# Gated linear scans in a decoder layer: all eight sample states of a head multiplied in one run of passes, and three blocks of values turned by 32x32 blocks and DMAs in place of TensorE transposes

## The chip, the cores and the metric

One core of one Trainium2 chip runs the whole program. The metric is the device time of one execution in microseconds (us). The kernel before takes 2281.77 us, the median of three runs (2281.49 to 2285.34). The engines are named as in the profile: PE (TensorE; PEld is its loading of weights), DVE (VectorE), ACT (ScalarE), POOL (GpSimd) and SP (SyncE, which here only issues DMAs).

## The reference

One layer with two feed-forward blocks (FFN1, FFN2) and between them a mixer of recurrent heads, for 256 prompt tokens and for 32 sample tokens (8 sequences of 4). The mixer has 4 GLA heads (keys of 128, values of 256) and 8 HGRN heads (keys of 128, values of 128). Each head is a scan with its own state S of keys by values:

```python
S_t = diag(a_t) S_{t-1} + k_t^T v_t      # a_t, k_t, q_t: 128 wide; v_t: 256 or 128 wide
o_t = q_t S_t
```

The prompt starts from a zero state. Each of the 8 sample sequences starts from a state of its own, which is an input, so a head has eight sample states. Outputs are the layer's result for both groups of tokens and the final states. The projections are `h @ w_in`, where values v are one part of the columns.

## The kernel before, in words

**Layout.** Activations lie with features on the 128 partitions and the 288 tokens (256 prompt, 32 sample) along the free axis: 16 tiles `x`, 16 tiles `y`, and for the matmuls `xh` and `xl`, the high and low part of x. Weights arrive over SP's queue in units of 512 KB (`raw`), ACT rounds each into `wh` (L96), DVE makes the rest `wl` (L97), and each product is three matmuls of 288 columns (L548, L549, L550). `Weights` keeps 3 raw units and 4 split units ahead.

**Order.** `block` (L539) computes 512 output features: for each of 16 input tiles k it issues 4 x 3 = 12 matmuls, then calls `tick(k)`. In the mixer, `tick` (L1284) carries the scans along under the projections: it takes one item from `turns`, then advances the first scan's generator one step, then runs what `later` holds. So a step of a scan stands in PE's queue between two groups of 12 matmuls. The queues of the engines are in order; a framework lays out the instructions of each engine from the program's order and sets the semaphores.

**Blocks in the mixer.** qk0, v0, qk1, v1 for the two GLA pairs of heads, then hfq0, hi0, hfq1, hi1, hfq2, hfq3 for the four HGRN pairs, then four gate blocks. v0, v1, hi0 and hi1 make the values, 512 features each, and each scan works on two heads (a = 0, 1). The six scans run under the block after the one that completes their inputs.

**Values** (`ev_v`, L882). The scans need values with tokens on the partitions. As each of a block's four feature tiles f is done, DVE multiplies its 256 prompt columns by the norm `rt` into a tile y (L887) and three copies of its 32 sample columns into `v3` (L888), and one turn is put on `turns`. A turn is three PE transposes into a PSUM tile `tp_v` (L866 twice, L867 for the three copies), an ACT copy into `Vt` (L895), an ACT copy of the sample part into `V32` (L896), and the stacked high, low and high parts `Vs` (ACT L871, DVE L873). With four blocks there are 16 turns.

**Scan** (`scan`, L910). Eight levels build the decayed scores (`Dg`, `Ds`, `X`). From the third last step on, and at each sample step, `load_state` (L929) puts one 256 KB DMA of sample states on SP's queue: 2 states for GLA, 4 for HGRN, 5 buffers in all. Then for each of the two heads:

- `out(a)` (L1158): PE multiplies values and scores into `po` for the prompt, and into `ss` for the samples (L1169 stands last of these).
- `sample(a, b0)`, four times for GLA (2 states each) and twice for HGRN (4 states each): the update `sn` from keys and values (L1191 or L1194); for each state b a product of the queries `qm` (32 columns as weights) with the state (256 or 128 columns) into `ss` on the 32 partitions of b % 4 (L1198); then DVE's new state (L1202) and its DMA out on POOL's queue (L1204).
- `final(a)`, `inter_a`, `inter_b`, `norm_a`: the prompt's final state, and the sum of the four groups of partitions of `ss`.

All operands of L866, L867, L1169, L1178 and L1198 are full 32-bit floats. One such matmul of L1169, L1178 or L1198 in the program appears as two in the trace (two passes); a transpose appears as one. So the 12 heads with 8 states each give 96 matmuls at L1198, 192 in the trace.

**32x32 turning in FFN2.** FFN2 has a second way to turn a tile, which the change brings to the mixer: DVE transposes each 32x32 block in place (`turn32`, L657; L660 and L662), and DMAs then carry the blocks to their rows (`move32`, L664), 16 for the prompt columns of four tiles, in 32 partitions x 8 runs of 32 floats each.

Of the kernel before, what the change touches and what calls it, by code (L numbers as in the profile page):

```python
# [16 lines left out]
P = 128  # L17
# [108 lines left out]
def trunk_kernel(ctx, tc, x_prompt, x_sample, state_gla, state_hgrn, norm_gains, f1_in, f1_out, f2_in, f2_out,  # L126
# [649 lines left out]
    def mixer(pn, border):  # L776
        with ExitStack() as mx:
# [84 lines left out]

            def by_token(tp, src, src3):

                for t in range(2):
                    PE.transpose(tp[:, t * P:(t + 1) * P], src[:, t * P:(t + 1) * P], ident)  # L866
                PE.transpose(tp[0:96, TP:TP + P], src3, ident)  # L867

# [6 lines left out]
            def vtiles(nm):  # L875
                vs32.append(vs32.pop(0))
                return (gp.tile([P, 2, 512], F32, name=f"V{nm}", tag="V"), vs32[-1],
                        gp.tile([96, 512], F32R, name=f"Vs{nm}", tag="Vs"))

            turns = []  # L880

            def ev_v(Vt, V32, Vs, y0=8):  # L882
                def ev(f, ps):

                    vt = y[y0 + f]
                    v3 = tmp.tile([P, 3, TS], F32, name="v3", tag="v3", bufs=4)
                    V.tensor_tensor(vt[:, 0:TP], ps[:, 0:TP], rt[:, 0:TP], op=ALU.mult)  # L887
                    V.tensor_tensor(v3, ps[:, TP:T].unsqueeze(1).broadcast_to([P, 3, TS]),  # L888
                                    rt[:, TP:T].unsqueeze(1).broadcast_to([P, 3, TS]), op=ALU.mult)

                    def turn():
                        tp = auxtile("tp_v")
                        by_token(tp, vt, v3.rearrange("p n t -> p (n t)"))
                        c = slice(f * P, (f + 1) * P)
                        S.activation(Vt[:, 0:2, c], tp[:, 0:TP].rearrange("p (t c) -> p t c", c=P), AF.Copy)  # L895
                        S.activation(V32[0:TS, c], tp[0:TS, TP:TP + P], AF.Copy)  # L896
                        stack(Vs[:, c], tp, TS)

                    turns.append(turn)
                return ev  # L900
# [9 lines left out]
            def scan(d, Vt, V32, Vs, gla, ytile0, s0, sp_out, ss_out):  # L910
# [18 lines left out]
                def load_state():  # L929
                    if loads:  # L930
                        a, b0 = loads.pop(0)
                        t = sp[0].tile([P, nb, dv], F32, name="s0", tag="s0", bufs=5)
                        with tc.issue_after(W.last[W.loaded - 3]):
                            nc.sync.dma_start(t, s0[b0:b0 + nb, a].rearrange("b p v -> p b v"))
                        states[a, b0] = t
# [156 lines left out]
                for step in range(LEVELS + 1):  # L1092
# [32 lines left out]
                    if step == 3:  # L1125
                        for a in range(2):
# [31 lines left out]
                def out(a):  # L1158
                    vc = Vt[:, :, a * dv:(a + 1) * dv]

                    po, ss = auxtile("o"), auxtile("os")
                    for j in range(nv):
                        vj = vc[:, :, j * P:(j + 1) * P]
                        c0, c1, c2 = j * TP, j * TP + P, (j + 1) * TP
                        PE.matmul(po[:, c0:c1], vj[:, 0, :], Dg[:, 0, a, :], start=j == 0, stop=True, skip_group_check=True)
                        PE.matmul(po[:, c1:c2], vj[:, 0, :], X[:, a, :], start=False, stop=False, skip_group_check=True)
                        PE.matmul(po[:, c1:c2], vj[:, 1, :], Dg[:, 1, a, :], start=False, stop=True, skip_group_check=True)
                        c0 = TP + j * TS
                        PE.matmul(ss[:, c0:c0 + TS], V32[:, a * dv + j * P:a * dv + (j + 1) * P], Ds[:, a, :],  # L1169
                                  start=j == 0, stop=False, skip_group_check=True)  # L1170
                    pos[a] = po, ss

                def final(a):

                    kd, vc = kds[a][0], Vt[:, :, a * dv:(a + 1) * dv]
                    ps = auxtile("st")
                    for t in range(2):
                        PE.matmul(ps[:, 0:dv], kd[:, t, :], vc[:, t, :], start=t == 0, stop=t == 1)  # L1178
                    st = tmp.tile([P, dv], F32, name="st", tag="st", bufs=1)
                    S.activation(st, ps[:, 0:dv], AF.Copy)  # L1180
                    G.dma_start(sp_out[a], st)

                def sample(a, b0):
# [9 lines left out]
                    else:  # L1193
                        PE.matmul(ps, ks, bd.rearrange("p b c -> p (b c)"), start=True, stop=True)  # L1194
                    for i in range(nb):
                        b = b0 + i
                        r = slice(b % 4 * TS, (b % 4 + 1) * TS)
                        PE.matmul(pos[a][1][r, 0:dv], qm[a][:, b * TS:(b + 1) * TS], s[:, i, :],  # L1198
                                  start=False, stop=b >= NB - 4, skip_group_check=True)
                    for i in range(nb):  # L1200
# [163 lines left out]
            for g in range(2):  # L1364
                d = group_tiles(f"g{g}")
                block(f"qk{g}", KT, xrhs, ev_gla(d, g == 0), tick=tick if g else pn.tick0, most=99 if g else 1,
                      fill=None if g else border.fill)
                if g == 0:
                    scan_pool()
                if g == 0:  # L1370
                    vt = vtiles("g0")
                    block("v0", KT, xrhs, ev_v(*vt), 
                          tick=lambda k: (pn.tick1(k), split_lr() if k == 8 else a_lr() if k == 13 else None))
                    lower_bounds()
                    gla_decay(d, g)
                else:
                    gla_decay(d, g)
                    vt = vtiles("g1")
                    block("v1", KT, xrhs, ev_v(*vt), tick=tick)
                gens.append((g, scan(d, *vt, True, 4 * g, state_gla[0][:, 2 * g:2 * g + 2],  # L1380
                                     sgp[0, 0, 2 * g:2 * g + 2], sgs[0][:, 2 * g:2 * g + 2]), True))
            ds, vts = {}, {}
            for kind, g in HORDER:
                if kind == "hi":
                    written(g)
                    vts[g] = vtiles(f"h{g}")
                    block(f"hi{g}", KT, xrhs, ev_v(*vts[g], 8 + 4 * g), tick=tick)
                else:
# [3 lines left out]
                for j in list(ds):  # L1392
                    if j // 2 in vts:
                        c = slice((j % 2) * 256, (j % 2 + 1) * 256)
                        vt, v32, vs = vts[j // 2]
                        gens.append((2 + j, scan(ds.pop(j), vt[:, :, c], v32[:, c], vs[:, c], False, 8 + 2 * j,
                                                 state_hgrn[0][:, 2 * j:2 * j + 2], shp[0, 0, 2 * j:2 * j + 2],
# [113 lines left out]
```

## Time and profile before

The profiled execution took 2281.72 us. Its span, from the first to the last instruction, is 2279.5 us.

| what | before |
|---|---|
| median of three runs | 2281.77 us |
| profiled execution, span | 2281.72 us, 2279.5 us |
| granted TensorE clock | 0.998 |
| DVE busy | 1397.6 us (61%) |
| ACT busy | 1015.4 us (45%) |
| POOL busy | 134.6 us (6%) |
| DMA mean | 168 GB/s |

The mixer takes roughly 900 to 1300 us of the span. A row of a group reads: line, engine, operation, output<-inputs, shapes, count, then busy us, mean ns of one, and idle time before. A row of the timeline reads: start in us, length in us, engine, line, operation and count; matmuls overlap, so what one costs is read from the distance between starts, and the length is modelled.

### The profile page before, as it was taken

To read this page: it belongs to the slowest core of one execution; us is meant where nothing else is said; L and a number is where in the kernel's file an instruction comes from. 1 tells how busy PE (TensorE), PEld (TensorE's weight loads), DVE (VectorE), ACT (ScalarE), POOL (GpSimd) and SP (SyncE) were. 2 spreads that over 40 slices of the span, in tenths; PEclk is the share of its full clock that TensorE was granted. 3 is DMA by queue.
4 is the path that set the end of the run, shared out by engine and by line. 5 is a ranking of instruction groups with operands and counts; after the bars stand their busy time and mean duration, and the time that the engine had idled before them with its cause. 6 is when DMAs were issued, how large, how long until landed. Compare 5 with 4: busy or idle time off the path is not lost.

```text
span 2279.5 us, 42047 instructions
## 1 busy us (share of the span) xinstructions
PE 2265.8 (99%) x17216; PEld 2240.5 (98%) x17216; DVE 1397.6 (61%) x2293; ACT 1015.4 (45%) x1539; POOL 134.6 (6%) x241
## 2 busy tenths in 40 slices
PE   9999999999999999999999999999999999999998
PEld 9999999999999999999999999999999999999998
DVE  7545545554555468778878754954555455545546
ACT  6443333333334346555556654644333333333344
POOL 2000000000000002001000000340000000000005
PEclk9999999999999999999999999999999999999999
DMA  7555555445555544556565554565555555455445
GB/s 218 169 167 166 167 167 165 166 165 166 166 165 184 167 158 148 165 160 186 156 172 169 160 185 158 157 191 166 167 167 166 167 167 165 164 168 165 165 164 157
DMA packets 225601, 382.43 MB, mean 168 GB/s; under 512 B 20242, under 2 KB 60224, under 8 KB 225408
## 3 DMA queue, kind: packets, MB, share of 16 engines
q1 hardware_dynamic: 214736, 365.15, 49.9%
q0 software_dynamic: 8496, 14.41, 2.3%
q8 instruction: 135, 2.21, 0.4%
q10 hardware_dynamic: 2176, 0.18, 0.1%
q14 instruction: 58, 0.48, 0.1%
HBM read 363.75 MB, written 11.80 MB: 165 GB/s over the span
## 4 chain that ended last, share of the span: by engine, by line
PE 97%; DVE 1%; ACT 0%; issue 0%; DMA 0%; DVEq 0%; SPq 0%; POOL 0%; ACTq 0%; POOLq 0%
PE gate L548 10%; PE gate L550 10%; PE gate L549 10%; PE up L550 8%; PE up L548 8%; PE up L549 8%; PE out L549 8%; PE out L550 8%; PE out L548 8%; PE mo L550 1%; PE hfq L548 1%; PE mo L548 1%; PE mo L549 1%; PE hfq L549 1%; PE hfq L550 1%; PE hi L548 1%
## 5 line engine op out<-in xcount | busy, mean ns | idle before, releaser
L97 DVE TENSOR_TENSOR wl<-raw,wh 128x1024 fp32r<-128x1024 f32 (+1 forms) x674 | 821.5, 1219 | 631.4 <-ACT wh L96 627.1
L96 ACT ACTIVATE wh<-raw 128x1024 fp32r<-128x1024 f32 (+1 forms) x674 | 711.8, 1057 | 1036.1 <-PE gate L549 318.1
L550 PE MATMUL gate<-xh,wl 128*128 128x288 f32 x1660 | 489.1, 295 | 0.5 <-DVE wl L97 0.5
L548 PE MATMUL gate<-xh,wh 128*128 128x288 f32 x1660 | 489.1, 296 | 0.1
L549 PE MATMUL gate<-xl,wh 128*128 128x288 f32 x1660 | 485.8, 295 | 0.4 <-DVE xl L255 0.4
L549 PE MATMUL out<-hl,wh 128*128 128x288 f32 x1408 | 415.6, 295 | 0.0
L550 PE MATMUL up<-xh,wl 128*128 128x288 f32 x1408 | 415.1, 295 | 0.0
L550 PE MATMUL out<-hh,wl 128*128 128x288 f32 x1408 | 415.0, 295 | 0.0
L548 PE MATMUL up<-xh,wh 128*128 128x288 f32 x1408 | 414.8, 295 | 0.0
L549 PE MATMUL up<-xl,wh 128*128 128x288 f32 x1408 | 414.6, 294 | 0.0
L548 PE MATMUL out<-hh,wh 128*128 128x288 f32 x1408 | 413.8, 294 | 0.3 <-DVE u L626 0.3
L548 PEld LDWEIGHTS gate<-xh,wh 128*128 128x128 f32 x1660 | 310.9, 188 | 1.9 <-issue 1.0
L550 PEld LDWEIGHTS gate<-xh,wl 128*128 128x128 f32 x1660 | 311.6, 188 | 1.1 <-DVE wl L97 1.0
L549 PEld LDWEIGHTS gate<-xl,wh 128*128 128x128 f32 x1660 | 310.4, 188 | 0.9 <-DVE xl L255 0.6
L548 PEld LDWEIGHTS out<-hh,wh 128*128 128x128 f32 x1408 | 264.6, 188 | 0.6 <-DVE u L626 0.6
L550 PEld LDWEIGHTS out<-hh,wl 128*128 128x128 f32 x1408 | 264.7, 188 | 0.0
L548 PEld LDWEIGHTS up<-xh,wh 128*128 128x128 f32 x1408 | 264.1, 188 | 0.4 <-ACT g L618 0.3
L549 PEld LDWEIGHTS out<-hl,wh 128*128 128x128 f32 x1408 | 264.4, 188 | 0.0
L549 PEld LDWEIGHTS up<-xl,wh 128*128 128x128 f32 x1408 | 264.2, 188 | 0.1
L550 PEld LDWEIGHTS up<-xh,wl 128*128 128x128 f32 x1408 | 264.2, 188 | 0.0
L706 DVE TENSOR_TENSOR y<-out,y 128x288 f32<-128x288 f32 x288 | 121.0, 451 | 101.3 <-PE out L550 98.3
L548 PE MATMUL hfq<-xh,wh 128*128 128x288 f32 x256 | 78.1, 305 | 0.0
(382 smaller groups left out, 2544.0 us busy)
## 6 DMA issues: line engine op xcount, KB each, us to landing
raw<-in_ffn_w_in_dram SPq DMA_DIRECT2D x351, 512.0 KB, 3.4
raw<-in_ffn_w_out_dram SPq DMA_DIRECT2D x176, 512.0 KB, 3.5
raw<-in_mix_w_in_dram SPq DMA_DIRECT2D x64, 512.0 KB, 3.7
raw<-in_mix_w_in_dram SPq DMA_DIRECT2D x96, 256.0 KB, 3.1
raw<-in_mix_w_out_dram SPq DMA_DIRECT2D x32, 512.0 KB, 3.6
out_dram<-s POOLq DMA_DIRECT2D x32, 256.0 KB, 3.1
s<-in_state_gla_dram SPq DMA_DIRECT2D x16, 256.0 KB, 4.1
s<-in_state_hgrn_dram SPq DMA_DIRECT2D x16, 256.0 KB, 5.0
```

The source lines that it names most:

```text
L96: i1 = self.nc.scalar.activation(h[:, c], raw[:, c], AF.Copy).ins
L97: i2 = self.nc.vector.tensor_tensor(l[:, c], raw[:, c], h[:, c].bitcast(F32), op=ALU.subtract).ins
L548: yield lambda: PE.matmul(dst, w[0][:, c:c + P], parts[0], start=start, stop=False)
L549: yield lambda: PE.matmul(dst, w[0][:, c:c + P], parts[1], start=False, stop=False)
L550: yield lambda: PE.matmul(dst, w[1][:, c:c + P], parts[0], start=False, stop=stop)
L706: V.tensor_tensor(y[k], ps, y[k], op=ALU.add)
```

## The change

1. `sample` no longer multiplies the states with the queries. `out(a)` does it, for all eight states of the head in one run of eight matmuls right behind L1169. `load_state` gets 8 buffers in place of 5 and begins one step earlier (`LEVELS - 4`).
2. In the blocks v0, v1 and hi0 the values are not turned by PE. DVE multiplies all 288 columns at once into one of four grouped tiles `yg`, and eight turns replace the four: two `turn32` (DVE, two tiles each, the second also the sample columns of all four), four `move32` on POOL's queue (20 DMAs per block, 4 of them for the samples), one empty, and `parts`, which makes `Vs` for the whole block from `V32` by two ACT copies and one DVE subtraction of 32x512.
3. hi1 is still turned by PE, but its third transpose takes 32 columns in place of 96 (the three copies are gone), and `Vs` comes from `parts`.
4. The 16 tiles y become slices of four tiles; `Vt` is laid out by feature tile, then token half. The final state's matmul reads it with a stride.

```diff
-    y = [xpool.tile([P, T], F32, name=f"y{k}") for k in range(KT)]
+    yg = [xpool.tile([P, 4, T], F32, name=f"y{k}") for k in range(4)]
+    y = [yg[k // 4][:, k % 4, :] for k in range(KT)]
...
-            def ev_v(Vt, V32, Vs, y0=8):
+            def ev_v(Vt, V32, Vs, g, spare):
+                vg = yg[g]
+                if spare is not None:
+                    flat = yg[spare].rearrange("p f c -> p (f c)")
+                    b32 = flat[:, 0:4 * TP].rearrange("p (q n c) -> p q n c", q=4, c=TS)
+                    bs32 = flat[:, 4 * TP:].rearrange("p (f c) -> p f c", c=TS)
...
+                def turn32(f):
+                    def run():
+                        for i in (f, f + 1):
+                            V.transpose(b32[:, :, 2 * i:2 * i + 2, :], vg[:, i, 0:TP].rearrange("p (t q c) -> p q t c", t=2, q=4))
+                        if f:
+                            V.transpose(bs32, vg[:, :, TP:T])
+                    return run
+
+                def move32(b, sample):
+                    rows = cols = slice(b * TS, (b + 1) * TS)
+                    def run():
+                        if sample:
+                            for n in range(4):
+                                r = slice(n * TS, (n + 1) * TS)
+                                G.dma_start(V32[0:TS].rearrange("p (f c) -> p f c", c=P)[:, :, r], bs32[r])
+                        for q in range(4):
+                            G.dma_start(Vt[q * TS:(q + 1) * TS, :, :, cols].rearrange("p f t c -> p (f t) c"), b32[rows, q])
+                    return run
+
+                def parts():
+                    v = V32[0:TS, :]
+                    S.activation(Vs[0:TS, :], v, AF.Copy)
+                    V.tensor_tensor(Vs[TS:2 * TS, :], v, Vs[0:TS, :].bitcast(F32), op=ALU.subtract)
+                    S.activation(Vs[2 * TS:96, :], v, AF.Copy)
+
                 def ev(f, ps):
-                    vt = y[y0 + f]
-                    v3 = tmp.tile([P, 3, TS], F32, name="v3", tag="v3", bufs=4)
-                    V.tensor_tensor(vt[:, 0:TP], ps[:, 0:TP], rt[:, 0:TP], op=ALU.mult)
-                    V.tensor_tensor(v3, ps[:, TP:T].unsqueeze(1).broadcast_to([P, 3, TS]),
-                                    rt[:, TP:T].unsqueeze(1).broadcast_to([P, 3, TS]), op=ALU.mult)
...
-                    turns.append(turn)
+                    V.tensor_tensor(vg[:, f, :], ps, rt, op=ALU.mult)
+                    if spare is None:
+                        turns.append(by_engine(f))
+                    if f == 3:
+                        if spare is not None:
+                            turns.append(turn32(0))
+                            turns.append(turn32(2))
+                            turns.extend(move32(b, b == 0) for b in range(4))
+                            turns.append(lambda: None)
+                        turns.append(parts)
...
-                        t = sp[0].tile([P, nb, dv], F32, name="s0", tag="s0", bufs=5)
+                        t = sp[0].tile([P, nb, dv], F32, name="s0", tag="s0", bufs=8)
...
-                    if step >= LEVELS - 3:
+                    if step >= LEVELS - 4:
                         load_state()
...
                 def out(a):
...
+                    for b in range(NB):
+                        r = slice(b % 4 * TS, (b % 4 + 1) * TS)
+                        PE.matmul(ss[r, 0:dv], qm[a][:, b * TS:(b + 1) * TS], states[a, b // nb * nb][:, b % nb, :],
+                                  start=False, stop=b >= NB - 4, skip_group_check=True)
...
                 def sample(a, b0):
...
-                    for i in range(nb):
-                        b = b0 + i
-                        r = slice(b % 4 * TS, (b % 4 + 1) * TS)
-                        PE.matmul(pos[a][1][r, 0:dv], qm[a][:, b * TS:(b + 1) * TS], s[:, i, :],
-                                  start=False, stop=b >= NB - 4, skip_group_check=True)
...
-                    block("v0", KT, xrhs, ev_v(*vt), 
+                    block("v0", KT, xrhs, ev_v(*vt, 2, 1), 
...
-                    block("v1", KT, xrhs, ev_v(*vt), tick=tick)
+                    block("v1", KT, xrhs, ev_v(*vt, 2, 1), tick=tick)
...
-                    block(f"hi{g}", KT, xrhs, ev_v(*vts[g], 8 + 4 * g), tick=tick)
+                    block(f"hi{g}", KT, xrhs, ev_v(*vts[g], 2 + g, None if g else 3), tick=tick)
```

More of the change, by code (lines that the diff above doesn't have):

```diff
@@ L861, in group_tiles, with by_token @@
                 return {n: gp.tile([P, 2, T], F32, name=f"{n}_{nm}", tag=n) for n in ("q", "k", "f")}
-            def by_token(tp, src, src3):
+            def by_token(tp, src, src3=None):
                 for t in range(2):
                     PE.transpose(tp[:, t * P:(t + 1) * P], src[:, t * P:(t + 1) * P], ident)
-                PE.transpose(tp[0:96, TP:TP + P], src3, ident)
+                n = TS if src3 is None else 3 * TS
+                PE.transpose(tp[0:n, TP:TP + P], src[:, TP:T] if src3 is None else src3, ident)
             def stack(dst, tp, low):
@@ L876, in vtiles @@
                 vs32.append(vs32.pop(0))
-                return (gp.tile([P, 2, 512], F32, name=f"V{nm}", tag="V"), vs32[-1],
+                return (gp.tile([P, 4, 2, P], F32, name=f"V{nm}", tag="V"), vs32[-1],
                         gp.tile([96, 512], F32R, name=f"Vs{nm}", tag="Vs"))
             turns = []
-            def ev_v(Vt, V32, Vs, y0=8):
-                def ev(f, ps):
-                    vt = y[y0 + f]
-                    v3 = tmp.tile([P, 3, TS], F32, name="v3", tag="v3", bufs=4)
-                    V.tensor_tensor(vt[:, 0:TP], ps[:, 0:TP], rt[:, 0:TP], op=ALU.mult)
-                    V.tensor_tensor(v3, ps[:, TP:T].unsqueeze(1).broadcast_to([P, 3, TS]),
-                                    rt[:, TP:T].unsqueeze(1).broadcast_to([P, 3, TS]), op=ALU.mult)
[L891 to L897, printed above, removed]
-                    turns.append(turn)
```

17 lines of the change are left out of this document (12 added, 5 removed).

## The prediction

> **What bounds the kernel now.** First the page's busy shares and its chain of work that ended last; then, for the mixer (910 to 1300 us), what PE's weight loads waited for, because a stage of its own may have a limit of its own.
>
> ```profile
> PE 2265.8 (99%) x17216; PEld 2240.5 (98%) x17216; DVE 1397.6 (61%) x2293; ACT 1015.4 (45%) x1539; POOL 134.6 (6%) x241
> ...
> PE 97%; DVE 1%; ACT 0%; issue 0%; DMA 0%; DVEq 0%; SPq 0%; POOL 0%; ACTq 0%; POOLq 0%
> ```
>
> ```profile
> PEld os L1198 <- issue: 3.0, 12, 0.3
> ...
> PEld os L1198 <- DMA raw<-in_mix_w_in_dram: 0.5, 2, 0.3
> ```
>
> PE is busy 99% of the span and is 97% of the chain. In the mixer no DMA holds it for more than 0.5 us in all, and the largest entry, 3.0 us of "issue" at L1198, is no wait for data: 12 short pauses ahead of the matmuls that the change moves. So a microsecond of PE work taken out of the mixer comes off the time, as long as nothing else becomes late. What a piece costs PE is the distance between starts around it.
>
> **1. Transposes that go.** PE's timeline around one turn of v0:
>
> ```profile
> 916.39 0.29 PE L550 MATMUL qk<-xh,wl 128*128 128x288 f32 x1
> 916.52 0.38 PE L866 MATMUL tp_v<-ident,y 128*128 128x128 f32 x2
> 916.74 0.27 PE L867 MATMUL tp_v<-ident,v 128*96 128x128 f32 x1
> 916.76 0.38 PE L548 MATMUL qk<-xh,wh 128*128 128x288 f32 x1
> 916.98 0.30 PE L549 MATMUL qk<-xl,wh 128*128 128x288 f32 x1
> 917.12 0.29 PE L550 MATMUL qk<-xh,wl 128*128 128x288 f32 x1
> ```
>
> From the L550 at 916.39 to the L549 at 916.98 are 0.59 us, for two ordinary steps of 0.13 (the last two rows: 0.14) and three transposes. So a turn costs 0.59 - 0.26 = 0.33, or 0.11 a transpose. Three blocks of four turns go: 12 x 0.33 = **3.9 us**. hi1 keeps its four turns; their third transpose has 32 columns of weights in place of 96. Of that form there is FFN2's tail:
>
> ```profile
> 2268.64 0.60 PE L688 MATMUL tp_s<-ident,z 128*32 128x128 f32 x4
> 2269.08 0.39 PE L403 MATMUL postf<-onesD,sq 128*128 128x1 f32 x3
> ```
>
> Four in 0.44, so 0.11 each as before: nothing.
>
> **2. State matmuls before.** A GLA run of two states (four passes), a GLA run of four states (two samples that happen to stand together), and an HGRN run of four states:
>
> ```profile
> 961.22 0.40 PE L1191 MATMUL sn<-Vsg,bd 96*128 96x256 f32 x2
> 961.55 0.63 PE L1198 MATMUL os<-s,qm 128*32 128x256 f32 x4
> 962.10 0.40 PE L548 MATMUL v<-xh,wh 128*128 128x288 f32 x1
> 962.34 0.29 PE L549 MATMUL v<-xl,wh 128*128 128x288 f32 x1
> ...
> 1023.17 0.64 PE L1198 MATMUL os<-s,qm 128*32 128x256 f32 x8
> 1023.74 0.40 PE L548 MATMUL hi<-xh,wh 128*128 128x288 f32 x1
> 1023.97 0.29 PE L549 MATMUL hi<-xl,wh 128*128 128x288 f32 x1
> ...
> 1102.03 0.40 PE L1194 MATMUL sn<-bd,ks 96*128 96x512 f32 x1
> 1102.36 0.43 PE L1198 MATMUL os<-s,qm 128*32 128x128 f32 x8
> 1102.72 0.40 PE L548 MATMUL hi<-xh,wh 128*128 128x288 f32 x1
> 1102.95 0.29 PE L549 MATMUL hi<-xl,wh 128*128 128x288 f32 x1
> ```
>
> Four states of 256 columns take 0.57 us to the next matmul (1023.17 to 1023.74), two take 0.55: the groups of partitions work side by side, and most of a run is its beginning and end (the step behind it is 0.24 in place of 0.13). From sn to the second matmul after the run are 1.12 us (961.22 to 962.34). Without the run there would be two passes of 256 columns and one step; scaling 0.133 for 288 columns, 2 x 0.118 + 0.133 = 0.37 (an estimate). So a GLA run costs 0.75, an HGRN run 0.92 - (0.236 + 0.133) = 0.55. GLA has 4 heads x 4 samples, of which two stand in one run, so 15 runs: 11.3 us. HGRN has 8 x 2 = 16 runs: 8.8 us, of which I take off 0.1 for the one that already follows L1169. Before: **20.0 us**.
>
> **3. State matmuls after.** They stand behind L1169, where one HGRN run stands already. Beside it, an L1169 with no run behind it:
>
> ```profile
> 1018.55 0.31 PE L1169 MATMUL os<-Ds,vs 128*128 128x32 f32 x2
> 1018.70 0.38 PE L548 MATMUL hfq<-xh,wh 128*128 128x288 f32 x1
> 1018.91 0.30 PE L549 MATMUL hfq<-xl,wh 128*128 128x288 f32 x1
> ...
> 1198.13 0.39 PE L1167 MATMUL o<-Dg,Vh 128*128 128x128 f32 x2
> 1198.36 0.31 PE L1169 MATMUL os<-Ds,vs 128*128 128x32 f32 x2
> 1198.59 0.43 PE L1198 MATMUL os<-s,qm 128*32 128x128 f32 x8
> 1198.95 0.40 PE L548 MATMUL gate<-xh,wh 128*128 128x288 f32 x1
> 1199.18 0.29 PE L549 MATMUL gate<-xl,wh 128*128 128x288 f32 x1
> ```
>
> 0.82 (1198.36 to 1199.18) less 0.36 (1018.55 to 1018.91) is 0.46 for four states of 128 columns, with no estimate in it. The second four come as two more passes on the same four groups; a pass of 128 columns takes 0.11 (1198.13 to 1198.36, two passes). So an HGRN head costs 0.46 + 0.22 = 0.68, eight 5.5. For 256 columns the run of 1023.17 was 0.21 longer than that of 1198.59 (0.57 against 0.36), so 0.105 more per pass: a GLA head costs 0.46 + 0.21 + 2 x 0.215 = 1.10, four 4.4. After: **9.9 us**, 10.1 less.
>
> No run in the trace has one group twice, so the second four are bounded: at best the passes alone (taken: the four groups' passes follow each other without a break inside each run above); at worst they cost a whole run of their own, 8 x 0.92 + 4 x 1.34 = 12.7.
>
> **4. DVE, ACT, SP.** Per turned block DVE loses four pairs of multiplications and four subtractions and gains four multiplications, five transposes and one subtraction; ACT loses twelve copies and gains two. DVE is not on the chain, and the nearest cover is the split weights, of which four units (4 x 24 matmuls x 0.133 = 12.8 us of PE work) lie ready: nothing, and up to that cover if a wait in ACT (two copies in `parts` wait for the sample DMAs, with wh queued behind them) grows. The states of a head must now all be there at `out`. In SP's queue the loads had stood for their buffers:
>
> ```profile
> SPq L934 <- DMA out_dram<-s: 20.4, 6, 5.7
> ```
>
> With eight buffers and one step more of lead that 20.4 us goes and the raw loads behind it move up. I cost the earlier need at nothing, since no state load holds PE now and the loads come earlier by what they waited; the other end is the longest of these waits once in each of the two GLA scans, 11 us.
>
> **5. The moves.** 20 DMAs per block go to POOL, each ahead of every state output queued behind, and PE's first `out` now waits for the last. FFN2's moves of the same shape (ns of one, first and last start; us to landing), and the stretch in which 80 of them ran against the stretch after it (us; PE, PEld, DVE, ACT and POOL busy; clock, DMA share, GB/s):
>
> ```profile
> L671 POOL DMA_DIRECT2D xT<-b x64: 582/582/602, 1459.6 to 1511.2; - x64
> ...
> xT<-b POOLq DMA_DIRECT2D x64, 32.0 KB, 3.7
> ...
> 1450.00:1530.00 80.00, 79.97 (x599) 79.40 (x599) 55.67 (x104) 39.92 (x61) 45.86 (x81) 1.00 0.69 204
> 1530.00:1610.00 80.00, 80.00 (x606) 80.00 (x605) 38.75 (x47) 36.07 (x52) 0.00 (x0) 1.00 0.49 162
> ```
>
> 80 DMAs in 52 us is 0.65 each, with PE busy 79.97 of 80; they raised the DMA share by 0.20. So 20 moves take 13 us and land about 4 us later (3.7). The room is least in hi0:
>
> ```profile
> 1060.12 0.25 DVE L888 TENSOR_TENSOR v<-hi,rt 128x96 f32<-128x96 f32 x1
> ...
> 1085.35 0.38 PE L1165 MATMUL o<-Dg,Vh 128*128 128x128 f32 x2
> ```
>
> 25 us from the last multiplication to `out`, less some 2 for the transposes; 17 are needed. Hidden, by 6 us. The first state output behind them on POOL belongs to a sample step after `out`, so it waits for none of them.
>
> There is a rule against this. The Trainium skill, "SBUF — State Buffer", section "SBUF: two separate sides", says that a DMA issued from POOL starves while VectorE holds the port pair the two share, and its section "A bandwidth-pool intuition that's wrong" puts a 620 ns DMA at about 3100 ns so. By that the 20 moves would take 62 us and end far behind `out`. The rows above show 582 to 602 ns with DVE 70% busy (55.67 of 80), so here the trace does not show it.
>
> **Sum.** 3.9 + 10.1 = 14.0 us off the profiled execution's own 2281.72 (0.05 below the median, so no correction): **2267.7 us**, 0.6% faster.
>
> **Rivals.**
>
> *The second four states do not overlap.* For: a group of partitions must finish its state before the next. Against: passes of one group follow without a gap today. Saving 20.0 - 12.7 + 3.9 = 11.2: 2270.5.
>
> *The moves are late (slower).* Each move waits for one of DVE's long operations before POOL can issue it. The longest that is common:
>
> ```profile
> L97 DVE TENSOR_TENSOR wl<-raw,wh 128x1024 fp32r<-128x1024 f32 (+1 forms) x674 | 821.5, 1219 | 631.4 <-ACT wh L96 627.1
> ```
>
> Then a move takes 0.58 + 1.22 = 1.8, twenty 36, with landing 40 us, against the 23 of hi0, taken for all three blocks: PE stands 3 x 17 = 51 us, less 14 saved: 2319. It decides from three delays of 4.7 us on, which is 27.7 us for moves and landing, 1.2 us a move: nearly twice what the trace shows. Against it: the 64 moves took at most 602 ns to issue. For it: no such moves stand in the mixer yet, where other work of DVE lies beside them. The rule under 5 names the same mechanism.
>
> *States or moves late by a little.* 5 to 11 us of PE waits in all (the end named under 4) give 2273 to 2279; beyond 2277.2 that is no change.
>
> *The run brings nothing*, because what a run costs is not in entering and leaving it: only the transposes are saved, 2277.8. The rows at 961.55 and 1023.17 speak against it, so it shares the chance of the third.
>
> **How the numbers follow.** Forecast 0.70, second four apart 0.12, a little late or no gain from the run 0.10, moves late 0.08. What a measurement of this kernel can tell from no change is 0.2%, 4.6 us: below 2277.2 is faster. The forecast, its neighbour and half of the third are below (0.87), 0.05 is within, 0.08 above. The range for 8 in 10 takes the first two with the estimate of 0.37 off by 0.1 in each of 31 runs (3 us): 2264.5 to 2274.
>
> **What would show it.** Right: no tp_v in v0, v1 and hi0; 12 runs of 16 passes, an HGRN run some 0.58 us from its first start to the next matmul (0.36 + 0.22), a GLA run 1.0; PE's busy time down by about as much as the span. Wrong: PE waiting for a DMA at L1203 (`out`'s first matmul) or L1212 (the moved state matmuls); POOL's moves well over 0.65 us apart; runs of 0.7 and 1.2 us.

## The result, and the profile after

The changed kernel took 2272.32 us (median of 5 runs, 2270.91 to 2273.11) against 2281.77 of the kernel before: ratio 0.9951, interval 0.9939 to 0.9964. That is 9.5 us less where 14.0 were forecast; the direction and the range held, the size is two thirds of the forecast, and 2272.32 is 4.6 us above the 2267.7 of the sum. The profiled execution took 2270.91 us with a span of 2269.1.

The page of the changed kernel, engines' busy time and the chain of work that ended last:

```profile
PE 2253.5 (99%) x17180; PEld 2237.0 (99%) x17180; DVE 1394.7 (61%) x2280; ACT 1011.9 (45%) x1507; POOL 169.1 (7%) x301
...
PE 95%; DVE 2%; DMA 1%; issue 1%; ACT 1%; POOL 0%; DVEq 0%; ACTq 0%; POOLq 0%; SPq 0%
```

PE's busy time is down by 12.3 us, but the span by 10.4, and PE's share of the chain fell from 97% to 95%, with DVE and DMA in its place. Work did go from PE, and something else is now late. To see where, I take one stretch, from PE's first matmul of qk behind v (913 us) to its first of mo (1310): 10.1 of the 10.4 us lie between these two matmuls. The windows view of the two kernels over it (us; PE, PEld, DVE, ACT and POOL busy; clock, DMA share, GB/s), before and after:

```profile
913.34:1319.85 406.51, 405.81 (x3213) 384.37 (x3212) 324.79 (x721) 229.79 (x508) 30.18 (x44) 1.00 0.56 168
```

```profile
912.91:1309.32 396.41, 393.50 (x3176) 380.72 (x3175) 321.61 (x710) 226.39 (x475) 64.63 (x104) 1.00 0.60 176
```

10.1 us less. PE idled 0.7 us in the stretch before and 2.9 after, so 2.2 of the 3.9 us that are missing to the forecast's 14.0 are idle time. The other 1.7 are work that did not go: PE's busy time fell by 12.3. The waits view of PE (us in total, times, longest) over 905 to 1310 names that idle time; before and after:

```profile
PE sc L1067 <- DVE k_g L1014: 0.3, 1, 0.3
PE sc L1067 <- DVE k_h L1014: 0.3, 1, 0.3
```

```profile
PE sc L1105 <- DVE k_g L1052: 1.6, 1, 1.6
PE sc L1071 <- ACT R L1064: 1.0, 1, 1.0
```

Both are waits for the scan's own chain, one in the scan of v0 and one in that of hi0, and neither is for a move or a state. (A scan runs under the projections of the next block, so PE's matmuls around these two are those of qk and of hfq.) The first, traced back over the timelines of DVE and ACT in v0:

```profile
923.11 0.63 ACT L923 ACTIVATE Vsg<-vs 32x512 fp32r<-32x512 f32 x1 [1.35 <-DMA vs<-y]
923.76 0.63 ACT L925 ACTIVATE Vsg<-vs 32x512 fp32r<-32x512 f32 x1
```

```profile
923.77 0.68 DVE L924 TENSOR_TENSOR Vsg<-vs,Vsg 32x512 fp32r<-32x512 f32 x1 [1.01 <-ACT Vsg L923]
924.49 0.46 DVE L1049 TENSOR_TENSOR Q<-Q,F 128x288 f32<-128x288 f32 x1
...
932.94 0.41 DVE L1052 TENSOR_TENSOR k_g<-k_g,F 128x256 f32<-128x256 f32 x1
```

```profile
931.58 0.29 PE L551 MATMUL qk<-xh,wl 128*128 128x288 f32 x1
933.50 0.97 PE L1105 MATMUL sc<-Q,k_g 128*112 128x64 f32 x8 [1.62 <-DVE k_g L1052]
934.27 0.38 PE L549 MATMUL qk<-xh,wh 128*128 128x288 f32 x1
```

The first copy of `parts` (L923) waits 1.35 us in ACT for the samples' DMAs. DVE's subtraction of `parts` (L924) waits for that copy, 1.01 us, and takes 0.68. Everything that DVE does for the scan from there on stands behind it, down to k_g, and PE's score matmuls wait for k_g. From the start of L551 to that of L1105 are 1.9 us; the view, which models the end of L551, calls 1.62 of them idle. Below, a gap is the distance between starts. PE stands still though weights for the next units are there: the qk matmuls at 934.27 start as soon as the scores are out of the way, because in PE's queue they stand *behind* them. In hi0 the wait of L923 is 1.82 us and PE's gap 1.31, and there it is ACT's own copy of R that stands behind `parts`:

```profile
1060.81 0.63 ACT L923 ACTIVATE Vsh<-vs 32x512 fp32r<-32x512 f32 x1 [1.82 <-DMA vs<-y]
...
1062.44 0.42 ACT L1064 ACTIVATE R<-Q 128x256 f32<-128x256 f32 x1
```

The runs of state matmuls are what was forecast. An HGRN and a GLA head on PE's timeline:

```profile
1189.08 0.31 PE L1207 MATMUL os<-Ds,vs 128*128 128x32 f32 x2
1189.31 0.65 PE L1212 MATMUL os<-s,qm 128*32 128x128 f32 x16
1189.89 0.40 PE L549 MATMUL gate<-xh,wh 128*128 128x288 f32 x1
```

```profile
969.72 1.07 PE L1212 MATMUL os<-s,qm 128*32 128x256 f32 x16
970.72 0.40 PE L549 MATMUL v<-xh,wh 128*128 128x288 f32 x1
```

16 passes in 0.58 us and in 1.00, with no wait ahead of them; the second four states follow the first without a break. And the moves, on POOL's timeline of v0:

```profile
917.38 0.63 POOL L918 DMA_DIRECT2D Vg<-y  x1 [7.28 <-DVE y L906]
918.00 2.20 POOL L916 DMA_DIRECT2D vs<-y  x4
920.19 6.90 POOL L918 DMA_DIRECT2D Vg<-y  x12
```

0.55 to 0.63 us each. These are the four DMAs of the samples and 13 of the sixteen moves.

### The profile page after: what moved, and what is told of

It is laid out like the page before. It is cut to its first block, busy times and chain, and to the rows that moved or that the text cites. A ratio compares the mean times of both kernels' runs of the same rounds, so it can differ in the third digit from the quotient of the medians.

```text
span 2269.1 us, 42003 instructions
## 1 busy us (share of the span) xinstructions
PE 2253.5 (99%) x17180; PEld 2237.0 (99%) x17180; DVE 1394.7 (61%) x2280; ACT 1011.9 (45%) x1507; POOL 169.1 (7%) x301
## 4 chain that ended last, share of the span: by engine, by line
PE 95%; DVE 2%; DMA 1%; issue 1%; ACT 1%; POOL 0%; DVEq 0%; ACTq 0%; POOLq 0%; SPq 0%
PE gate L549 9%; PE gate L551 9%; PE gate L550 9%; PE out L550 8%; PE out L551 8%; PE out L549 8%; PE up L551 8%; PE up L549 8%; PE up L550 8%; PE mo L551 1%; PE mo L549 1%; PE mo L550 1%; PE hfq L549 1%; PE hfq L550 1%; PE hfq L551 1%; PE v L549 1%
## 5 line engine op out<-in xcount | busy, mean ns | idle before, releaser
L551 PE MATMUL gate<-xh,wl 128*128 128x288 f32 x1660 | 488.8, 295 | 0.5 <-DVE wl L97 0.5
L551 PE MATMUL up<-xh,wl 128*128 128x288 f32 x1408 | 415.1, 295 | 0.0
L551 PE MATMUL out<-hh,wl 128*128 128x288 f32 x1408 | 415.0, 295 | 0.0
L551 PEld LDWEIGHTS gate<-xh,wl 128*128 128x128 f32 x1660 | 311.5, 188 | 0.9 <-DVE wl L97 0.9
L551 PEld LDWEIGHTS out<-hh,wl 128*128 128x128 f32 x1408 | 264.7, 188 | 0.0
L551 PEld LDWEIGHTS up<-xh,wl 128*128 128x128 f32 x1408 | 264.2, 188 | 0.0
```

Of the source, the lines that this page charges most:

```text
L551: yield lambda: PE.matmul(dst, w[1][:, c:c + P], parts[0], start=False, stop=stop)
```

## The experiments

My theory after reading the traces (A): the forecast's gains are there, and what is missing is lost in waits for `parts` at the head of the scan's chain. The rival (B): `parts` is a bystander, and the transposes on VectorE, the moves, or the run of eight brought less than forecast. Four kernels first, five rounds each, beside a kernel before of 2283.91 us.

**e1_parts_late**: `parts` of the three turned blocks moves behind the last copy of the scan's set-up.

```diff
                         if spare is not None:
...
-                            turns.append(lambda: None)
-                        turns.append(parts)
+                            prep.append(parts)
+                        else:
+                            turns.append(parts)
...
-                put(LEVELS - 1, pss.pop(LEVELS - 1))
+                copied = put(LEVELS - 1, pss.pop(LEVELS - 1))
+                if prep:
...
+                    with tc.issue_after(copied):
+                        prep.pop(0)()
```

> The samples' values of v0, v1 and hi0 are put in place (parts) at the end of the scan's set-up, behind the last copy of X, instead of at its start. Theory A: what the changed kernel gained short of the forecast is TensorE waiting for the scan's own chain, because parts on ScalarE and VectorE waits for the samples' DMAs at the head of that chain (ScalarE idle for 1.82 us in hi0 and 1.35 in v0 ahead of its copy, TensorE then idle for 1.31 us at 1062.9 and 1.91 at 933.5). By A the gap in hi0 goes (1.3) and that in v0 shrinks to the 0.6 that stood there before (1.3): 2269.7 against 2272.3 of the changed kernel, and at least 1.3 faster if the gap in v0 has another cause. Rival B: the two gaps come from the transposes on VectorE or from contention with the moves, and parts is a bystander: 2272.3, within 0.5.

**e2_run_only**: `ev_v` of v0, v1 and hi0 with `spare` None, so that PE turns them; the run of eight stays.

> Only the run of eight states is kept; all four blocks of values are turned by TensorE as before. By the forecast's terms this saves the 10.1 us of the state matmuls alone: 2271.7. Theory A: the transposes' 3.9 us are for the most part given back by TensorE's new waits in v0 and hi0, so that this kernel takes as long as the changed one: 2271 to 2273. Rival B: the turning brings its 3.9 and it is the run of eight that fell short (by some 3 to 4 us): 2275 to 2276, slower than the changed kernel by 3 to 4.

**e3_turn_only**: the state matmuls go back from `out` into `sample`; the turning stays.

> Only the turning is kept; the state matmuls are back in two or four runs for each head, where they were. Theory A: the transposes' 3.9 us go and some 3 come back as waits for the scan's chain: 2280 to 2281.5, against 2281.8 of the kernel before. Rival B: turning brings its 3.9: 2277.9.

**e4_samples_last**: the samples' DMAs behind the sixteen moves.

```diff
-                            turns.extend(move32(b, b == 0) for b in range(4))
+                            turns.extend(move32(b, b == 3) for b in range(4))
```

(and inside `move32` the moves ahead of the samples)

> The four DMAs of the samples' values are issued behind the sixteen moves instead of ahead of them, so that parts, and what is queued behind it on ScalarE and VectorE, waits for some 9 us more (sixteen moves of 0.58). Theory A: the scan's chain is late by that in v0 and hi0 and TensorE runs out of the other work there: slower than the changed kernel by 5 to 18 us (2277 to 2290), with TensorE's idle time at the scan's first score matmuls of v0 and hi0. Rival B: TensorE has enough split weights to go on with and parts is a bystander: 2272.3, within 0.5.

Measured, with the stretch of 913 to 1310 us from each trace, worked out as the difference to the 406.51 of before:

```
kernel            us       ratio to before (interval)   stretch
changed (own)     2272.32  0.9951 (0.9939 to 0.9964)    -10.1
e1_parts_late     2271.13  0.9945 (0.9931 to 0.9958)    -12.4
e2_run_only       2274.24  0.9958 (0.9946 to 0.9971)     -8.9
e3_turn_only      2284.41  1.0001 (0.9992 to 1.0010)     +1.4
e4_samples_last   2270.66  0.9942 (0.9929 to 0.9954)    -13.1
```

The expectations were written against the 2281.8 of the first comparison, so times of the two comparisons are held against each other by their ratios. e3 says it most plainly: turning by itself, with 3.9 us of transposes gone, brings nothing (A had expected 0.3 to 1.8 us). Its waits of PE:

```profile
PE sc L1105 <- DVE k_g L1052: 1.9, 2, 1.6
PE sc L1071 <- ACT R L1064: 1.4, 1, 1.4
PE sc L1105 <- DVE k_h L1052: 1.2, 1, 1.2
```

4.5 us of waits for the scan's chain, against 0.6 before: more than the transposes were worth. A further part of e3's loss is a lower clock behind the first of these gaps (0.50 from 936.19 to 939.60; the last section comes back to it). In e2, where PE turns, no wait is listed in the stretch. Its 2274.24 lies between the two theories as it stands (A: 2271 to 2273, B: 2275 to 2276) and in A's range by its ratio (2272.2 of 2281.77), and its interval overlaps that of the changed kernel, so the clock settles little here. Its stretch is 8.9 us shorter where 10.1 were forecast for the run of eight. So B has a part too: with no wait at all, the run brought 1.2 us less than the forecast. e1's gap in hi0 is gone, and in v0 there is none over 0.40; its only wait in the stretch is another, in the scan after:

```profile
PE sc L997 <- ACT R L989: 0.6, 1, 0.6
```

So A explains e1 and e3, with a gain of 2.3 us of e1 over the changed kernel in the stretch where 2.6 were expected, and most of what is missing, but not the 1.2 of e2. By the clock e1 and the changed kernel are not told apart here: their intervals overlap.

e4 contradicted A on its face: the samples come later, and the kernel got no slower (5 to 18 us were expected). The timeline of ACT in hi0 shows why it was no test:

```profile
1062.71 0.40 ACT L1064 ACTIVATE R<-Q 128x256 f32<-128x256 f32 x1
...
1072.29 0.63 ACT L923 ACTIVATE Vsh<-vs 32x512 fp32r<-32x512 f32 x1
```

The order of the engines' queues is drawn up at build time, and with later samples the build put `parts` behind the scan's copy of R, 10 us further back: e4 is a second e1, not a longer wait. So the next four keep e4 as their foot and one of them holds `parts` where it was. Beside a kernel before of 2282.97 us:

**a_again**: the changed kernel itself.

> The changed kernel once more, beside the next three on one chip. It stood at 2272.3 in its own comparison (ratio 0.9951), and the kernel with the samples' DMAs last at 2270.7 in another (0.9942). 2272 if the two stand on the same footing, and again TensorE gaps of some 1.9 and 1.3 us at the first score matmuls of v0 and hi0.

**e5_two_fours** (on e4): the second four states in a run of their own.

```diff
                 def out(a):
...
-                    for b in range(NB):
+                    for b in range(4):
...
                 def sample(a, b0):
...
+                    if b0 == 4:
+                        for b in range(4, NB):
+                            r = slice(b % 4 * TS, (b % 4 + 1) * TS)
+                            PE.matmul(pos[a][1][r, 0:dv], qm[a][:, b * TS:(b + 1) * TS], states[a, b // nb * nb][:, b % nb, :],
+                                      start=False, stop=True, skip_group_check=True)
```

> Built on the kernel with the samples' DMAs last (2270.7). States 0 to 3 of a head run in out, states 4 to 7 in a run of their own in the sample step that loads the second four, so that entering and leaving a run of column groups is paid twice a head. Theory A (a run's price is entering and leaving it, as the forecast has it): HGRN 0.55 in place of 0.22 for the second four (8 heads, 2.6 us), GLA 0.75 to 0.9 in place of 0.43 (4 heads, 1.3 to 1.9): 3.9 to 4.5 us more, 2274.6 to 2275.2. Rival B (the price goes by matmuls or passes, and the gain of the eight came from somewhere else): 2270.7, within 0.7.

**e6_parts_first** (on e4): what is left of `turns`, up to `parts`, is run ahead of the scan's copy of R, and that copy is held behind the last copy of `parts`.

```diff
...
-                    S.activation(near, src, AF.Copy)
+                    while early:
+                        turns.pop(0)()
+                    with tc.issue_after(pinned.pop()) if pinned else ExitStack():
+                        S.activation(near, src, AF.Copy)
...
```

> As the kernel with the samples' DMAs last (2270.7), but parts of v0, v1 and hi0 is held ahead of the scan's copy of R on ScalarE, where it stood in the changed kernel (in the kernel with the samples last it had slid behind that copy, so that it did not test the wait). parts now waits for the DMAs behind the sixteen moves, some 9 us later than in the changed kernel. Theory A (the scan's chain stands behind parts, and TensorE has little else to do there): gaps of TensorE of 6 to 11 us in each of v0 and hi0, and up to as much in v1: 2283 to 2300, slower than the kernel before the change. Rival B (the split weights at hand cover such a wait, as the forecast had it): 2270.7 to 2273.

**e7_moves_halved** (on e4): 32 moves a block in place of 16.

```diff
-                            G.dma_start(Vt[q * TS:(q + 1) * TS, :, :, cols].rearrange("p f t c -> p (f t) c"), b32[rows, q])
+                            for h in range(2):
+                                G.dma_start(Vt[q * TS:(q + 1) * TS, 2 * h:2 * h + 2, :, cols].rearrange("p f t c -> p (f t) c"),
+                                            b32[rows, q, 4 * h:4 * h + 4])
```

> As the kernel with the samples' DMAs last (2270.7), but each move is cut into two of half the size: 36 DMAs a block in place of 20. By the forecast's fifth step (a DMA holds its place by issue, 0.58 to 0.65 each, whatever its size, and room for 27 us in hi0): 36 x 0.62 = 22.3 and 4 to 5 to land, against some 23 us from the first issue (1055) to the first matmul of out in hi0 (1078): late by 3 to 5 us in hi0 and by nothing in v0 and v1: 2273.5 to 2276. Rival: moves of half the size go through in half the time, or other work hides the rest: 2270.7.

Measured:

```
kernel            us       ratio to before (interval)   stretch
a_again           2276.38  0.9965 (0.9952 to 0.9977)     -7.6
e5_two_fours      2273.30  0.9956 (0.9944 to 0.9969)     -9.0
e6_parts_first    2275.38  0.9962 (0.9948 to 0.9975)     -9.3
e7_moves_halved   2282.60  0.9998 (0.9989 to 1.0007)     +2.8
```

*e5*: 4.1 us more than e4 in the stretch, where 3.9 to 4.5 were expected. The runs in `out` are shorter by 0.22 in eight heads and by 0.43 in four, 3.5 us, so the twelve new runs cost 7.6, some 0.6 each. The passes are the same in number as in e4, so a price by passes (B) is out: most of a run's price is entering and leaving it. One of them, on PE's timeline:

```profile
1146.44 0.29 PE L551 MATMUL hfq<-xh,wl 128*128 128x288 f32 x1
1146.66 0.42 PE L1232 MATMUL os<-s,qm 128*32 128x128 f32 x8
1147.02 0.50 PE L1242 MATMUL sn<-bd,ks 96*128 96x512 f32 x1
1147.36 0.29 PE L1279 MATMUL hms<-nh,ones 128*128 128x288 f32 x1
```

0.22 us into it, 0.36 to the next matmul and 0.34 for that one, for four states that take 0.22 when they follow four others.

*e6*: slower than e4 by 3.8 us in the stretch. Its 2275.38 lies in neither range (A: 2283 to 2300, B: 2270.7 to 2273) and nearer to B: gaps of 6 to 11 us were expected by A, and the largest wait is 0.8:

```profile
PE sc L1078 <- ACT R L1071: 1.7, 3, 0.8
```

Three waits of R, one each in v0, v1 and hi0, where A has them, but short. The chain itself is late by far more. The first scores behind that copy of R in v0, in the changed kernel and in e6:

```profile
928.82 1.48 PE L1071 MATMUL sc<-R,k_g 128*128 128x192 f32 x8
```

```profile
939.95 1.57 PE L1078 MATMUL sc<-R,k_g 128*128 128x192 f32 x8 [0.41 <-ACT R L1071]
```

That is 15.9 us into the stretch (it begins at 912.91) and 23.6 (916.31): 7.7 later, and PE idles for 0.4 of it and fills the rest with further units. In the changed kernel (and in e4) 108 matmuls of qk stand ahead of these scores in the stretch, in e6 162: the build has put the score matmuls behind 54 more of them, 7.2 us at 0.133. So the units do cover such a wait, as the forecast had it, but only those of them that stand ahead of the waiting matmul in PE's queue. The waits of PE come to 2.4 of e6's 3.8 us; the rest was not followed.

*e7*: twice as many moves gave back the whole gain, 2282.60 where 2273.5 to 2276 were expected. PE's waits:

```profile
PE tp_k L867 <- DVE k_g L1054: 5.0, 1, 5.0
PE os L1209 <- DMA vs<-y: 2.8, 1, 2.8
PE sc L1107 <- DVE k_g L1054: 1.7, 1, 1.7
PE sc L998 <- ACT R L990: 0.9, 2, 0.6
PE o L1205 <- DMA Vh<-y: 0.5, 1, 0.5
```

The second and the last are the expected ones: in hi0 `out` is late by 0.5 + 2.8 = 3.3 us (3 to 5 expected). The first was not expected. It stands in v1, and over DVE and ACT it leads to `parts` again:

```profile
1014.87 0.68 DVE L926 TENSOR_TENSOR Vsg<-vs,Vsg 32x512 fp32r<-32x512 f32 x1 [6.75 <-ACT Vsg L925]
1015.58 0.43 DVE L1054 TENSOR_TENSOR k_g<-k_g,F 128x256 f32<-128x256 f32 x1
```

```profile
1014.21 0.63 ACT L925 ACTIVATE Vsg<-vs 32x512 fp32r<-32x512 f32 x1 [6.47 <-DMA vs<-y]
```

```profile
1010.85 0.29 PE L551 MATMUL hfq<-xh,wl 128*128 128x288 f32 x1
1016.15 0.66 PE L867 MATMUL tp_k<-ident,k_g 128*128 128x128 f32 x2 [5.01 <-DVE k_g L1054]
```

This is the test that e4 was meant to be: 6.5 us of waiting in ACT, 6.75 in DVE, 5.0 in PE, with hfq's units queued behind. All five waits of the list come to 10.9 of the 15.9 us by which e7's stretch is longer than e4's. The other 5.0 are PE's busy time, and in it the granted clock was 0.50 from 1014.88 to 1021.71 us, which begins within the first gap and ends 5.6 us behind it, and from 1089.97 to 1093.38, behind the second. The moves themselves take hardly less at half the size (0.55 each, by POOL's timeline in v0), so here a DMA's time on POOL goes by its issue and not by its bytes:

```profile
914.18 14.23 POOL L915 DMA_DIRECT2D Vg<-y  x26 [3.25 <-DVE y L904]
```

*a_again*: the changed kernel is slower than in its own comparison (2276.38, 0.9965; 2272 was expected), and its stretch is 2.5 us longer (-7.6 against -10.1). The gap of v0 is alike (1.89 us for 1.91), that of hi0 0.5 longer (1.84 for 1.31). What differs most is the clock behind the gap of v0. The windows view over 930 to 940 us, in a_again and in the first trace of the changed kernel:

```profile
930.00:940.00 10.00, 8.40 (x52) 7.74 (x51) 9.00 (x26) 2.77 (x5) 1.48 (x3) 0.83 0.76 213
```

```profile
930.00:940.00 10.00, 8.38 (x79) 7.74 (x79) 8.31 (x26) 3.03 (x5) 0.30 (x1) 1.00 0.74 223
```

The granted clock was 0.83 against 1.00, 52 matmuls were done in the time of 79. Within these 10 us it was 0.50 for 3.41 us:

```profile
936.69:940.10 3.41, 3.41 (x20) 3.13 (x21) 2.39 (x6) 0.00 (x0) 0.00 (x0) 0.50 0.40 142
```

A matmul of 288 columns took 0.24 us there from start to start where it takes 0.13:

```profile
937.20 0.44 PE L550 MATMUL qk<-xl,wh 128*128 128x288 f32 x1
937.44 0.44 PE L551 MATMUL qk<-xh,wl 128*128 128x288 f32 x1
```

Eleven such steps cost 11 x 0.11 = 1.2 us on top of the gap. The two traces have the same matmuls in the same order; held against each other one by one, a_again is 0.2 us behind at the scores that end the gap and 1.7 behind at the end of the slow piece, so it cost 1.5 in all.

Four kernels to close, beside a kernel before of 2282.72 us. **a_third** is the changed kernel, **e1_again** and **e4_again** are the two above, and **e8_turn_late** is e3 with e1's edit.

> The changed kernel a third time, as the foot for the next two. It stood at 2272.3 and at 2276.4 in two comparisons (8 to 11 us off the kernel before, by the ratios); the difference between those two was, for the most part, TensorE's waits in v0 and hi0. 2272 to 2276.

> parts at the end of the scan's set-up, once more, beside the changed kernel on one chip. Theory A (TensorE's waits in v0 and hi0 come from parts): 2.3 to 5 us faster than the changed kernel in this comparison, 12 to 13 off the kernel before. Rival B: within 1 of it.

> The samples' DMAs last, by which parts also slid behind the scan's chain; once more, beside the changed kernel on one chip. As with parts late: 3 to 5.5 us faster than the changed kernel, 13 off the kernel before. This or the kernel with parts late is the best version.

> Only the turning by VectorE and DMAs (the state matmuls as before), with parts at the end of the scan's set-up. With parts at its start the turning alone brought nothing (2284.4 against 2283.9 of the kernel before), though the transposes were to bring 3.9. Theory A (that 3.9 was there and was given back as waits behind parts): 3.5 to 4.2 faster than the kernel before, 2279 to 2280. Rival B (it is turning itself, by its transposes on VectorE or its DMAs, that costs the 3.9): no faster than the kernel before, 2283 to 2284.5.

```
kernel            us       ratio to before (interval)   stretch
a_third           2275.95  0.9967 (0.9955 to 0.9980)     -7.5
e1_again          2272.43  0.9950 (0.9938 to 0.9963)    -12.9
e4_again          2269.52  0.9940 (0.9926 to 0.9953)    -12.9
e8_turn_late      2278.35  0.9981 (0.9972 to 0.9989)     -4.6
```

e8 decides between A and B for the turning. Same transposes on VectorE, same moves, same DMAs as e3; only the place of `parts` differs, and turning alone goes from +1.4 to -4.6 us in the stretch, from no gain to 4.4 us (0.0019 of the time) by the clock, where A had expected 3.5 to 4.2. Of these 6.0 us, 4.3 are PE's idle time; the other 1.7 are PE's busy time, with the lower clock behind e3's gap among them. No wait is listed in e8's stretch. e1 and e4 are 3.5 and 6.4 us faster than the changed kernel beside them, and every run of theirs is faster than every run of it (2.3 to 5 and 3 to 5.5 were expected, and 12 to 13 off the kernel before, where e1 has 10.3 and e4 13.2); e4, at 2269.5, is the best version. e1 and e4 have the same stretch in this pair. What lies between their traces is outside of it: in e1_again PE's steps are 0.24 us for 15 matmuls at the start (24 to 28 us), and a gap at 1445 is 0.9 us longer than in e4_again. Neither place holds an edit, and why every run of e4_again was faster than every run of e1_again stays open.

## Why the prediction was right or wrong

The direction and the mechanism of the two gains were right; the step that failed is **step 4**, the change's cost on DVE, ACT and SP "at nothing". Of the 3.9 us that the first trace's stretch is short of 14.0, it accounts for 2.8 (2.2 of them idle time of PE); the other 1.1 are left even with `parts` out of the way, and the run of eight, which steps 2 and 3 took 1.2 too high by e2, is where they fit.

1. *Transposes that go*: 3.9 forecast, 4.6 measured (e8's stretch). The 0.7 more is in part the two waits of 0.3 that the kernel before had at L1067, which e8's waits no longer list. No run has hi1's narrower transpose alone; nothing in these sums asks for a cost of it.
2. and 3. *State matmuls*: 10.1 forecast, 8.9 measured (e2), or 12.9 - 4.6 = 8.3 as the part of e4_again that e8 has not. The runs themselves are right to 0.01 us (0.58 and 1.00), the second four do follow without a break, and e5 confirms the price of entering and leaving. By the forecast's own measure (from L1207 to the second matmul behind the run, less 0.36) an HGRN head costs 1.05 - 0.36 = 0.69 and a GLA head 1.48 - 0.36 = 1.12, in all 10.0 for the 9.9 of step 3. In step 2 the sixteen GLA samples lost 11.0 us, from sn to the second matmul behind it, for 11.3, and HGRN's twelve runs behind an sn 0.54 each for 0.55. Another 0.5 went into longer steps around sn that were not there before. So the 1.2 to 1.8 that are missing lie in no one place; what is left of them was not followed further.
4. *DVE, ACT, SP*: forecast 0, measured 2.8 in the first trace (12.9 of e1_again and e4_again, less 10.1) and 5.3 to 5.4 in the two later ones, where 1.5 and 1.4 of it are the lower clock behind the gap in v0. I had seen the wait of `parts` for the samples' DMAs and set the four ready units against it as cover. That cover was not where it was needed: the ready units stood behind the score matmuls that waited (the qk matmuls at 934.27 above), and e6 shows that those ahead do cover. e1_again, e4_again and e8 show the cause: with `parts` later these waits are gone. Nor was the thing to look at wh, "queued behind" the copies: it was the scan's own chain on DVE and ACT, one step further in the same two queues. The early need of the states, in the same step, was indeed free: no wait for a state is among PE's in any of these traces, and the 20.4 us that state loads stood in SP's queue for their buffers are gone (the changed kernel's state loads wait 1.8 us, for moves).
5. *The moves*: right. 16 moves and 4 samples were in time in all three blocks. e7 found the room in hi0 to be what was forecast (36 DMAs, issued from 1062.3 to 1085.7 by POOL's timeline, 0.65 each, made `out` 3.3 us late), so the rival "moves late" was a matter of twice as many DMAs, as its condition said. The rule of the Trainium skill weighed there ("SBUF — State Buffer", section "SBUF: two separate sides"), that DMAs issued from POOL starve while VectorE holds the shared port pair, does not show here either; whether VectorE held the pair beside these moves, no trace shows. The lines view of POOL over the changed kernel, for the 32 moves of v0 and v1 (busy us, mean ns of one):

```profile
L918 POOL DMA_DIRECT2D Vg<-y x32 | 18.6, 586 | 13.1 <-DVE y L906 7.3 <-issue 4.2 <-DMA Vg<-y 1.7
```

Of the rivals, *states or moves late by a little* is nearest in size, but what was late was neither a state nor one of the sixteen moves: it was the copy that waits for the samples' DMAs. With `parts` out of the way, e4_again's 2269.5 is 13.2 us off, near the forecast's 14.0, for a kernel that the change could have been; e1_again, with the same stretch, is 10.3 off.

That 2272.3 lies in the range is in part luck. The range was made for the second four and for the estimate of 0.37, and both came out as forecast; the waits that moved the time were in the sum at nothing. In the two later comparisons the same kernel stood at 0.9965 and 0.9967, which is 2273.8 and 2274.2 of 2281.77, at the edge of the range's 2274. The terms of step 1 and of steps 2 and 3 also miss in opposite directions (0.7 more, 1.2 to 1.8 less).

## What to carry to other kernels

In these traces, work that was ready covered a wait only where it stood ahead of the waiting instruction in that engine's queue; so ask of each new wait what follows it in its own queue, and then in the queues of those that follow. A helper's copy that waits for a DMA is best put behind the chain that feeds the bounding engine, where its result is still in time: here that was worth 3.5 us (e1_again). Work taken off a full engine is a gain only as long as no new wait takes its place: e3 took the transposes off PE and gained nothing, e8 kept 4.4 us.

## What the hardware showed beyond that

A gap in PE was followed by a lower clock in some executions and not in others. In a_again, a_third and e3 the gap of 1.9 us in v0 was followed by 3.41 us at a granted clock of 0.50; in the first trace of the changed kernel, with a gap as long, and in e7, with one of 2.0 us in v0, the clock stayed at 1.00. e7's gap of 5.3 us in v1 was followed by 6.83 us at 0.50, most of it behind the gap, and that of 3.1 in hi0 by 3.41. No trace without a gap of 1.9 us or more shows it in the stretch, and single gaps of up to 1.84 us elsewhere in the stretch were not followed by it. (At the start of the execution, e1_again and e6 have 3.41 us of it from 25 us on, behind two gaps of 1.0 to 1.4 us close together.) That the gap is the cause is read from these coincidences; no run set a gap on purpose.

The slow piece cost 1.5 us in a_again and 1.4 in a_third, more than half of the 2.5 and 2.6 us by which their stretches are longer than the first trace's. (The expectation of a_third put that difference down to waits for the most part.) The Trainium skill, "TensorE: Matmul & The Clock Gate", section "HAM oscillation — how this bites in real kernels", gives as the rule that no gap of PE should exceed about 3.4 us. Here 1.9 to 2.0 us were followed by the lower clock three times in five, so a gap below that bound is not safe; the same page's Part 1 says that the windows in which activity is counted run freely, which would fit that the same gap is punished in one execution and not in the next. No run here shows where the windows lay.
